# A two-block transformer layer on one core: sums over a convolution's channels by adding DMAs instead of GpSimd, and two pooling epilogues given out at two points

## The chip, the cores and the metric

The kernel runs on one core of a Trainium2 chip. The metric is the device time of one execution in microseconds (us). The engines are TensorE (PE, with its weight loads PEld), VectorE (DVE), ScalarE (ACT), GpSimd (POOL) and SyncE (SP). SP issues most DMAs; the DMAs that add to their destination are issued by POOL.

## The reference

The kernel computes two layers on 1024 positions of 1024 channels in float32. The change lies in the first one, in two of its three branches:

```
a_v, a_g, b_b, b_c, b_h, b_g, c_a, c_b, c_g, merge = split(u @ w_in + b_in)
pooled = causal_multiscale_pool(a_v)              # windows 2, 4, 8, 16, a group of 256 channels each
y_a = einsum("bsgi,gio->bsgo", pooled, pool_w) * pool_scale * silu(a_g)
h_c = causal_dwconv(c_a * sigmoid(c_b), cf_w, cf_b)           # 31 taps per channel
y_c = silu(layer_norm(h_c, cf_ln_g, cf_ln_b)) * silu(c_g)     # mean and variance over 1024 channels
m = sum over the three branches of sigmoid(merge_n) * (y_n @ w_branch[n])
```

The layer norm of `h_c` needs, for each position, the sum of `h_c` and of its square over all channels.

## The kernel before

Channels lie on partitions, 128 at a time, and positions along the free dimension, so a tile of 128x1024 is one block of 128 channels (512 KB). A float32 product is made of three products of split operands (`hilo`: a rounded part, cast by ACT, and a rest, subtracted by DVE; `mm3`). The host program writes every engine's queue in the order in which its calls are made; each engine then runs its queue in that order and waits where data or a buffer is not ready. A buffer that is used again is waited for by the next user's instruction.

The projections of the first layer run in two ways. The blocks j = 0 to 4 of the branches B and C are plain products (`slot_u`). All later projections go two blocks at a time through `run_two`, which makes seven half-size products out of eight (products 1, 6, 5, 2, 7, 3, 4 in that order, 12 matmuls each) and combines the results in PSUM by a copy on ACT and additions on DVE. ACT's copy `c1 = nc.scalar.copy(e[:, 0], banks[1])`, L456, takes the first product out of its bank. The fourth product writes that bank again and so waits for the copy; in the trace the copy is `two<-pp`. Work of the previous pair (its epilogue, `g.todo`, called `later` in the function) and of the background queue `bgq` is given out by `fill()`, which `run_two` calls after each product. A `Task` with a step k is not given out before k products have been made (`step * STEP > now[1] + 0.01`); it waits at the head of the list.

The convolution of a channel block j is done by DVE: `head`, L725, starts the tile `h`, and 30 `tap`s, L162, add to it. Then `stats()` stores `h`, squares it on ACT into a tile of the tag `e` (`sq`), and POOL adds `h` to `hs` and `sq` to `hq` (L740, L741). For j = 0 POOL copies instead. After j = 7 SP stores both sums to `st_sp` (L743, L744), from where they are read when the layer norm is due. The tag `e` is a small ring for results on the way to memory: two buffers (`n_e` = 2) while the convolutions run, one while the poolings run (`open_a` sets `n_e` = 1). The epilogues of projections (`epi_store`) use it too: an activation into `e`, L156, then a store.

The pooling products of a group g (`pool_slot`, g = 3, 2, 1, 0) are two PSUM pairs; their epilogues `one(0)` and `one(1)` scale a pair on ACT into a tile `e` and store it to `ya_sp`. For g = 0 they run at once and use other buffers, for the other three they are left to the next pair of `run_two`. In the last stage of the second layer, `down()` already uses adding DMAs on POOL (L1976, 256 KB each, from HBM).

Of the kernel before, what the change touches and what calls it, by code (L numbers as in the profile page):

```python
# [14 lines left out]
ALU = mybir.AluOpType  # L15
# [91 lines left out]
class Kernel:  # L107
# [603 lines left out]
    def block1(self):  # L711
        nc, I = self.nc, self.I
# [7 lines left out]
        def conv_tasks(j, p):  # L720
            w = lambda k: self.par("cf_w", j * 31 + k)

            def head():
                h = T["h"] = self.c0.tile([P, 1024], F, tag="h", name="h", bufs=2)
                nc.vector.tensor_scalar(h, p[:, 30:1054], w(30), self.par("cf_b", j),  # L725
                                        ALU.mult, ALU.add)

            def tap(k):
                self.stt(T["h"], p[:, k:k + 1024], w(k), T["h"], ALU.mult, ALU.add)

            def stats():
                h = T["h"]
                nc.sync.dma_start(h_sp[j], h)
                sq = e_tile()
                self.act(sq, h, AF.Square)
                if j == 0:
                    nc.gpsimd.tensor_copy(self.hs, h)
                    nc.gpsimd.tensor_copy(self.hq, sq)
                else:
                    nc.gpsimd.tensor_tensor(self.hs, self.hs, h, ALU.add)  # L740
                    nc.gpsimd.tensor_tensor(self.hq, self.hq, sq, ALU.add)  # L741
                if j == 7:
                    nc.sync.dma_start(st_sp[0], self.hs)  # L743
                    nc.sync.dma_start(st_sp[1], self.hq)  # L744

            self.bgq.append(Task(0.7, head))
            for k in range(30):
                self.bgq.append(Task(1.3, lambda k=k: tap(k)))
            self.bgq.append(Task(0, stats))

        def e_tile():
            return self.c1.tile([P, 1024], F, tag="e", name="e", bufs=self.n_e)
# [111 lines left out]
        pairs = Pairs(self.pair_tiles(lambda: self.cw, 1, True), lambda: None, lambda: None)  # L864
# [92 lines left out]
        def pool_slot(g):  # L957
            s = {}

            def pre():  # L960
                while self.bgq:
                    self.bgq.popleft()()
                pairs.flush()
                if g == 0:
                    self.open_right("ws")
                    self.resume()
                    self.dma_ahead()
                    for j in range(4):
                        split_y(1, j)
                    self.split_ahead(1)  # L970

            def mm():
                wh, wl = T["pwr"]
                s["ps"] = [self.pair(), self.pair()]
                for c in range(2):
                    for h in range(2):
                        hs = slice(h * H, (h + 1) * H)
                        for k in range(2):
                            ph, pl = T["pool", 2 * g + k]
                            ks = slice((k * 2 + c) * P, (k * 2 + c + 1) * P)  # L980
                            self.mm3(s["ps"][c][:, hs], (wh[:, ks], wl[:, ks]), (ph[:, hs], pl[:, hs]),
                                     k == 0, k == 1)

            def one(c):
                if g:
                    e = e_tile()
                else:
                    e = self.c1.tile([P, 1040], F, tag="s", name="s", bufs=2)[:, 0:1024]
                self.act(e, s["ps"][c], AF.Identity, scale=self.par("pool_scale", 2 * g + c))
                (nc.sync if g else nc.gpsimd).dma_start(ya_sp[2 * g + c], e)  # L990

            def epi():
                pairs.todo = [Task(0, lambda c=c: one(c)) for c in range(2)]
                if g == 0:
                    pairs.flush()

            self.slots.append(Slot([], mm, epi, pre=pre, name="pool%d" % g))

        def open_a():
# [35 lines left out]
        def split_y(n, j):  # L1035
            if ("Y", n) not in T:
                open_y(n)
            self.hilo(T["Y", n][0][:, j], T["Y", n][1][:, j], T["ld"].pop((n, j)))
# [1190 lines left out]
```

## Time and profile before

| what | before |
|---|---|
| median of 3 runs | 2711.1 us (2710.7 to 2712.61) |
| the profiled execution's own time | 2704.81 us |
| its span | 2703.0 us |
| mean granted TensorE clock | 0.994 |
| busy: PE, DVE, ACT, POOL | 97%, 70%, 36%, 7% of the span |

The span is the time from the first to the last instruction of the profiled execution. Busy shares are means over stages with different limits. The plain products of the first layer run up to about 376 us, the pairs of the first layer from there to about 1040 us.

### The profile page before, as it was taken

The page shows a single profiled execution, that of the slowest core. Times are in us where ns is not written, and L with a number is a line of the kernel's source. Part 1 is how long each engine was busy: PE and PEld are TensorE (multiplying, and loading weights), DVE is VectorE, ACT ScalarE, POOL GpSimd, SP SyncE. Part 2 cuts the span into 40 slices and gives each one's busy share as a digit, 9 for nine tenths or more (in the row PEclk, how much of TensorE's full clock was granted, in tenths as well). Part 3 has the DMA queues.
Part 4 walks back from the last instruction along what each step waited for, and adds up shares of the span by engine and source line. Part 5 has one row for each costly group of instructions (what it writes and reads, how often), then busy time and mean ns, then how long its engine had stood idle before and what let it go on. Part 6 is the DMA issues. An engine that isn't in the chain of part 4 may idle for free.

```text
span 2703.0 us, 29526 instructions
## 1 busy us (share of the span) xinstructions
PE 2622.2 (97%) x11688; PEld 2143.6 (79%) x11688; DVE 1881.6 (70%) x2141; ACT 981.1 (36%) x1284; POOL 182.4 (7%) x178
## 2 busy tenths in 40 slices
PE   5999999999999997999999999999999999999998
PEld 3888887888788776877887788888888888887776
DVE  7789988899886664566564254546647788885576
ACT  5322233333343333222243255542323334343333
POOL 4000000000000000000032100000000000000220
PEclk9999999999999998999999999999999999999999
DMA  6111121222232225676342121112532222216964
GB/s 234 55 63 63 63 86 70 102 86 94 86 129 109 99 108 186 255 287 253 125 156 83 68 86 65 68 32 100 180 130 78 86 79 85 88 61 234 276 147 149
DMA packets 102380, 324.63 MB, mean 120 GB/s; under 512 B 11489, under 2 KB 12001, under 8 KB 102242
## 3 DMA queue, kind: packets, MB, share of 16 engines
q1 hardware_dynamic: 95474, 309.65, 31.9%
q0 software_dynamic: 6768, 13.11, 2.6%
q8 instruction: 91, 1.49, 0.2%
q14 instruction: 47, 0.39, 0.0%
HBM read 247.21 MB, written 75.50 MB: 119 GB/s over the span
## 4 chain that ended last, share of the span: by engine, by line
PE 75%; DVE 10%; DMA 7%; ACT 4%; issue 3%; SPq 1%; POOL 1%; DVEq 0%; ACTq 0%; POOLq 0%
PE pp L143 73%; DMA A<-g_sp 1%; DVE h L162 1%; DMA B<-x_sp 1%; DVE sums L159 1%; DVE ld L159 1%; DVE wl L159 1%; DVE A L159 1%; PE pm L143 1%; DVE g L159 1%; DVE B L159 1%; ACT e L156 1%; PE pp L146 1%; PE pm L146 1%; DMA mg_sp<-e 1%
## 5 line engine op out<-in xcount | busy, mean ns | idle before, releaser
L143 PE MATMUL pp<-A,wh 128*128 128x512 f32 x2432 | 769.7, 392 | 13.5 <-DVE A L159 9.0
L143 PEld LDWEIGHTS pp<-A,wh 128*128 128x128 f32 x2432 | 454.4, 188 | 115.1 <-DVE A L159 10.9
L143 PE MATMUL pp<-A,wl 128*128 128x512 f32 x1296 | 506.0, 390 | 2.8 <-DVE wl L159 2.8
L143 PE MATMUL pp<-B,A 128*128 128x512 f32 x1676 | 487.8, 390 | 1.2 <-DVE B L159 1.1
L143 PE MATMUL pp<-A,w 128*128 128x512 f32 x1664 | 443.4, 392 | 12.8 <-DVE pp L159 6.7
L143 PEld LDWEIGHTS pp<-A,w 128*128 128x128 f32 x1664 | 313.7, 189 | 83.3 <-DVE pp L159 10.3
L143 PE MATMUL pp<-B,w 128*128 128x512 f32 x1136 | 374.7, 389 | 0.0
L143 PEld LDWEIGHTS pp<-B,A 128*128 128x128 f32 x1676 | 313.9, 188 | 68.1 <-DVE B L159 2.3
L162 DVE SCALAR_TENSOR_TENSOR h<-p,par_t,h 128x1024 f32<-128x1024 f32 x240 | 312.8, 1303 | 4.7
L143 PEld LDWEIGHTS pp<-A,wl 128*128 128x128 f32 x1296 | 243.8, 188 | 55.4 <-DVE wl L159 4.5
L143 PE MATMUL pp<-B,wh 128*128 128x512 f32 x800 | 263.8, 395 | 15.6 <-ACT B L165 8.3
L159 DVE TENSOR_TENSOR wl<-wr,wh 128x1024 fp32r<-128x1024 f32 (+1 forms) x120 | 144.3, 1203 | 172.7 <-ACT wh L165 168.8
L143 PEld LDWEIGHTS pp<-B,w 128*128 128x128 f32 x1136 | 213.2, 188 | 44.3
L143 PEld LDWEIGHTS pp<-B,wh 128*128 128x128 f32 x800 | 151.3, 190 | 49.3 <-ACT B L165 9.2
L165 ACT CAST wh<-wr 128x1024 fp32r<-128x1024 f32 (+1 forms) x120 | 118.5, 989 | 188.3 <-PE pp L143 159.2
L162 DVE SCALAR_TENSOR_TENSOR z<-pp,par_t,z 128x1023 f32<-128x1023 f32 x88 | 112.6, 1280 | 48.0 <-ACT z L156 47.0
L143 PE MATMUL pp<-yh,xh 128*128 128x512 f32 x308 | 122.6, 398 | 5.9 <-ACT yh L165 5.9
L373 ACT CAST w<-raw 128x1024 fp32r<-128x1024 f32 x50 | 52.6, 1053 | 207.8 <-PE pp L143 141.0
L143 PE MATMUL pp<-yl,xh 128*128 128x512 f32 x308 | 123.1, 400 | 4.4 <-DVE yl L159 4.4
L143 PE MATMUL pp<-A,A 128*128 128x512 f32 x324 | 126.7, 391 | 0.1
L143 PE MATMUL pp<-B,wl 128*128 128x512 f32 x320 | 125.9, 393 | 0.0
L143 PE MATMUL pp<-yh,xl 128*128 128x512 f32 x308 | 121.1, 393 | 0.0
(278 smaller groups left out, 3187.4 us busy)
## 6 DMA issues: line engine op xcount, KB each, us to landing
raw<-in_w_in SPq DMA_DIRECT2D x66, 512.0 KB, 4.1
wr<-in_w_in SPq DMA_DIRECT2D x63, 512.0 KB, 3.5
raw<-in_w_up SPq DMA_DIRECT2D x34, 512.0 KB, 5.2
mg_sp<-e SPq DMA_DIRECT2D x24, 512.0 KB, 4.1
wr<-in_w_br SPq DMA_DIRECT2D x24, 512.0 KB, 5.9
g<-mg_sp SPq DMA_DIRECT2D x24, 512.0 KB, 5.4
A<-g_sp SPq DMA_DIRECT2D x44, 256.0 KB, 6.3
g_sp<-z SPq DMA_DIRECT2D x21, 512.0 KB, 3.0
```

What stands on the lines that cost most here:

```text
L143: return self.nc.tensor.matmul(*a, **k)
L146: self.nc.tensor.transpose(*a)
L156: return self.nc.scalar.activation(out, in_, func, **kw)
L159: return self.nc.vector.tensor_tensor(out, a, b, op)
L162: self.nc.vector.scalar_tensor_tensor(out, a, s, b, op0, op1)
L165: self.nc.scalar.copy(hi, src)
L373: self.nc.scalar.copy(t.__dict__[which][0], src)
```

## The change

For j = 1 to 7 the two additions on POOL become two DMAs, issued by POOL, that read `h` or `sq` in SBUF and add it to `hs` or `hq` in SBUF. The two epilogues of a pooling get the steps 1 and 2: the first may be given out after one product of the next pair, the second after two.

```diff
                     nc.gpsimd.tensor_copy(self.hs, h)
                     nc.gpsimd.tensor_copy(self.hq, sq)
                 else:
-                    nc.gpsimd.tensor_tensor(self.hs, self.hs, h, ALU.add)
-                    nc.gpsimd.tensor_tensor(self.hq, self.hq, sq, ALU.add)
+                    nc.gpsimd.dma_start(self.hs, h, accum_op=ALU.add)
+                    nc.gpsimd.dma_start(self.hq, sq, accum_op=ALU.add)
                 if j == 7:
                     nc.sync.dma_start(st_sp[0], self.hs)
                     nc.sync.dma_start(st_sp[1], self.hq)
...
             def epi():
-                pairs.todo = [Task(0, lambda c=c: one(c)) for c in range(2)]
+                pairs.todo = [Task(0, lambda c=c: one(c), c + 1) for c in range(2)]
                 if g == 0:
                     pairs.flush()
```

ACT's queue at the start of the pair behind the pooling g = 2. The activations into `e` are `one(0)` and `one(1)`, the copy of L456 is `c1`, and the casts make weights of this pair and the next:

```order
 L373 CAST w_2393<-sums 128x1024 [waits PE_49]
 L156 ACTIVATE e<-pp,par_t 128x1024 [waits DMAHW6_49,PE_49,Activation_49]
-L156 ACTIVATE e<-pp,par_t 128x1024 [waits DMAHW7_49,PE_49,Activation_49]
-L456 COPY two<-pp 128x512 [waits PE_49]
+L456 COPY two<-pp 128x512 [waits PE_49]
+L156 ACTIVATE e<-pp,par_t 128x1024 [waits DMAHW7_49,Activation_49]
 L373 CAST w_2391<-raw 128x1024 [waits DMAHW3_49,PE_49]
 L373 CAST A_201<-sums 128x1024 [waits DVE_49]
```

The copy now stands ahead of `one(1)`; `one(0)` keeps its place. The poolings g = 3 and g = 1 read alike.

POOL's queue at the convolution blocks 1 and 2 (`q` and `p` are small memsets for the next blocks; a wait on DMASW is one for a DMA that POOL issued):

```order
 L780 MEMSET q 128x2 [waits Pool_49]
 L765 MEMSET p 128x30
-L740 TENSOR_TENSOR hs<-hs,h 128x1024 [waits DVE_49,Pool_49]
-L741 TENSOR_TENSOR hq<-hq,e 128x1024 [waits Activation_49,Pool_49]
+L740 DMA hs<-h 128x1024 [waits DVE_49,Pool_49]
+L741 DMA hq<-e 128x1024 [waits Activation_49,Pool_49]
 L780 MEMSET q 128x2 [waits Pool_49]
 L765 MEMSET p 128x30
-L740 TENSOR_TENSOR hs<-hs,h 128x1024 [waits DVE_49,Pool_49]
-L741 TENSOR_TENSOR hq<-hq,e 128x1024 [waits Activation_49,Pool_49]
+L740 DMA hs<-h 128x1024 [waits DMASW0_49,DVE_49]
+L741 DMA hq<-e 128x1024 [waits DMASW1_49,Activation_49]
```

Each addition is replaced at its place; from the second block on, a DMA also waits for the DMA that added to the same sum before.

ACT's queue at the pair behind block 5 (the two activations into `e` are the epilogue of two `merge` projections, the copy is `c1` of the pair):

```order
 L156 ACT_TABLE_LOAD [waits DMAHW5_49,DVE_49]
 L156 ACTIVATE e<-pp,par_t 128x1024 [waits Activation_49]
-L156 ACTIVATE e<-pp,par_t 128x1024 [waits Pool_49]
+L156 ACTIVATE e<-pp,par_t 128x1024 [waits DMASW1_49,Activation_49]
 L456 COPY two<-pp 128x512 [waits PE_49]
 L373 CAST w_2391<-raw 128x1024 [waits DMAHW7_49,PE_49]
```

Nothing moves here; the second activation's buffer held the square of block 5, and it is now released by the DMA's landing instead of POOL.

## Rows read from the trace of the kernel before

**Rows 1.** The page's first part: busy time, share of the span, instructions.
```profile
PE 2622.2 (97%) x11688; PEld 2143.6 (79%) x11688; DVE 1881.6 (70%) x2141; ACT 981.1 (36%) x1284; POOL 182.4 (7%) x178
```

**Rows 2.** What PE waited for, 82 to 1060 us: total, times, longest.
```profile
PE pp L143 <- DVE pp L159: 6.7, 4, 3.6
...
PE pp L143 <- ACT two L456: 5.9, 4, 2.4
```

**Rows 3.** Chain that ended last, 928 to 952 us: start, duration, what.
```profile
941.16 2.59 DMA ya_sp<-e
...
944.87 0.59 ACT two L456
```

**Rows 4.** PE's timeline behind the three poolings: start, duration, instruction, idle before.
```profile
880.30 3.04 PE L143 MATMUL pp<-A,w 128*128 128x512 f32 x12 [0.72 <-ACT two L456]
...
945.50 3.02 PE L143 MATMUL pp<-A,w 128*128 128x512 f32 x12 [2.27 <-ACT two L456]
...
1010.80 3.02 PE L143 MATMUL pp<-A,w 128*128 128x512 f32 x12 [2.39 <-ACT two L456]
```

**Rows 5.** POOL's timeline at convolution block 4.
```profile
463.25 2.42 POOL L740 TENSOR_TENSOR hs<-hs,h 128x1024 f32<-128x1024 f32 x1 [101.18 <-DVE h L162]
465.61 3.39 POOL L741 TENSOR_TENSOR hq<-hq,e 128x1024 f32<-128x1024 f32 x1
```

**Rows 6.** DVE's timeline: at block 4, and the same forms at 577 and 881 us.
```profile
463.69 3.06 DVE L159 TENSOR_TENSOR sums<-raw 128x1024 f32<-128x1024 f32 x1
466.67 2.94 DVE L725 TENSOR_SCALAR h<-p,par_t 128x1024 f32<-128x1024 f32 x1
...
577.55 0.80 DVE L725 TENSOR_SCALAR h<-p,par_t 128x1024 f32<-128x1024 f32 x1
...
881.49 1.22 DVE L159 TENSOR_TENSOR sums<-raw 128x1024 f32<-128x1024 f32 x1
```

**Rows 7.** PE's timeline behind the blocks 4, 5 and 6.
```profile
472.79 7.36 PE L143 MATMUL pp<-A,w 128*128 128x512 f32 x24 [3.62 <-DVE pp L159]
...
570.09 5.60 PE L143 MATMUL pp<-A,w 128*128 128x512 f32 x24
...
581.64 3.01 PE L143 MATMUL pp<-A,w 128*128 128x512 f32 x12 [0.51 <-ACT two L456]
...
688.40 3.90 PE L143 MATMUL pp<-A,w 128*128 128x512 f32 x9 [1.80 <-DVE pp L159]
```

**Rows 8.** One window by engine: length, busy and count each, granted clock, DMA.
```profile
472.50:476.50 4.00, 3.71 (x10) 2.96 (x11) 3.70 (x5) 0.00 (x0) 0.00 (x0) 0.63 0.00 0
```

**Rows 9.** The tile t of the last stage: duration in ns, least, median, most.
```profile
L1976 POOL DMA_DIRECT2D t<-in_w_dn x11: 865/875/1350, 2560.2 to 2611.3; - x11
...
L159 DVE TENSOR_TENSOR yl<-t,yh x11: 682/685/689, 2595.6 to 2625.8; 128x512 fp32r<-128x512 f32 x11
```

**Rows 10.** SP's issues behind convolution block 7.
```profile
799.11 0.32 SPq L744 DMA_DIRECT2D st_sp<-hq  x1
807.41 0.81 SPq L349 DMA_DIRECT2D raw<-in_w_in  x2
```

**Rows 11.** DMA queues: packets, MB, share of 16 engines' span.
```profile
q1 hardware_dynamic: 95474, 309.65, 31.9%
q0 software_dynamic: 6768, 13.11, 2.6%
```

**Rows 12.** POOL's DMA issues, 2587 to 2590 and 2473 to 2476 us: size, us to landing.
```profile
t<-in_w_dn POOLq DMA_DIRECT2D x1, 256.0 KB, 4.4
...
g_sp<-z POOLq DMA_DIRECT2D x1, 512.0 KB, 8.2
```

**Rows 13.** ACT's timeline behind block 5 (the first row is its square).
```profile
570.67 1.07 ACT L156 ACTIVATE e<-h 128x1024 f32<-128x1024 f32 x1 [4.00 <-issue]
...
578.99 2.12 ACT L156 ACTIVATE e<-pp,par_t 128x1024 f32<-128x1024 f32 x2
```

**Rows 14.** ACT's timeline behind block 4.
```profile
478.27 1.28 ACT L156 ACT_TABLE_LOAD   x1
```

## The prediction

> **What bounds the kernel now.** The first view is the page: TensorE (PE) is busy for 97% of the span [rows 1], so a change can pay only where PE stands still, or where it brings a stop of its own. The second view is the list of what PE waited for, cut to 82 to 1060 us, the stretch in which everything that the diff touches runs. Two causes matter there [rows 2]: 6.7 us for a VectorE (DVE) addition into `pp`, and 5.9 us for ScalarE's (ACT's) copy into `two`, the copy `c1` of `run_two`. The third and fourth views tell which stops these are.
>
> The copy first. In the chain that ended last, at 941 us, one reads a store `ya_sp<-e` and then the copy [rows 3]: the copy stands in ACT's queue behind the second pooling epilogue, that one waits until the first one's store has landed, because `e` has one buffer here, and PE waits for the copy. It happens after the three poolings g = 3, 2, 1, with idle times of 0.72, 2.27 and 2.39 us [rows 4].
>
> Now the addition. While GpSimd (POOL) adds `hs` and `hq`, for 2.42 and 3.39 us in the instance at 463 us [rows 5], two DVE instructions that begin meanwhile take 3.06 and 2.94 us; the same forms take 1.22 and 0.80 us elsewhere [rows 6]. So POOL's additions cost DVE (3.06 - 1.22) + (2.94 - 0.80) = 3.98 us here. PE then waits 3.62 us, and its next 24 matmuls take 7.36 us where 24 others take 5.60 [rows 7]: the granted clock is 0.63 over those 4 us, a mean of the levels 2.4 and 1.2 GHz [rows 8]. PE has the same pattern at 688 us, behind the channel block two later: 1.80 us idle, and 9 matmuls in 3.90 us [rows 7]. In the blocks 1 to 3 the additions run beside plain products, and the list has no such wait there.
>
> **The change part by part.** (a) *The two epilogues at two points.* The first stays where it was, ahead of the copy; the second goes behind the copy. The last matmul before the stop ends at 945.50 - 2.27 = 943.23 us [rows 4]. The first epilogue has ended by 941.16, when the store of its result begins [rows 3]; the copy of 0.59 us, whose product PE has computed long before, then ends near 941.8, 1.4 us before PE wants it. So the three idle times go: 0.72 + 2.27 + 2.39 = **5.4 us**. The second epilogue still waits for that store to land, at 941.16 + 2.59 = 943.75, and ends some 1.1 us later; behind it on ACT stands a cast into the buffer that PE reads in the fourth product, which begins at 943.2 and takes half of 5.60 us, so the cast can't start before 946 anyway, and nobody waits. SP issues its store at the same point of its queue as before.
>
> (b) *Fourteen additions leave POOL.* Seven pairs go, of which PE feels three. At 463 us: the DVE chain comes 3.98 us earlier, more than the 3.62 us of waiting, and with the idle time the slower clock goes: 3.62 + (7.36 - 5.60) = **5.4 us**. At 688 us: 9 matmuls at 5.60/24 = 0.233 us would be 2.1, so 1.80 + (3.90 - 2.10) = **3.6 us**. At 581 us the stop is 0.51 us [rows 7]; it is in (d). The margin at 463 us is 0.4 us, which is thin: I count the whole gain and put a smaller one among the rivals.
>
> (c) *Fourteen DMA issues come to POOL.* An issue of an adding DMA takes POOL 0.87 us, against the 2.4 to 3.4 us of an addition, and the eleven two-input DVE subtractions of the last stage, beside which such issues run, stay between 0.682 and 0.689 us [rows 9]. So I count no stretch of DVE. What stands behind them on POOL (the small memsets of `q`, `p`, `v`) comes earlier. On SP, the stores of `st_sp` now wait for landings instead of additions; the next issue in SP's queue, a load of `raw`, comes 8.3 us behind the second of them [rows 10], and that much lateness is covered.
>
> (d) *A later release of `e`.* `e` has two buffers here, and the square in one of them is now free when the DMA `hq<-e` has landed, not when POOL has added it. Who waits is an ACT activation, and in the blocks 4 to 7 the copy for PE stands right behind it. When does it land? No row shows an adding DMA of 512 KB between two places in SBUF. Its transfer time from the queues' totals [rows 11]: the hardware queue moved 309.65 MB in 31.9% of the span, so 0.524 MB take 1.46 us; the software queue 13.11 MB in 2.6%, 70.3 us; three plain 512 KB stores in it are 1.57 MB or 4.4 us, so adding costs 65.9 us for 11.5 MB, or **2.99 us** for 0.524 MB, twice a copy. Its fixed time lies between 4.4 - 1.5 = 2.9 us (an adding DMA of 256 KB after POOL had paused 25 us) and 8.2 - 1.46 = 6.7 us (a plain 512 KB DMA, the first after a long pause) [rows 12]. `hq` follows `hs` in one queue, so with T as the end of the block's convolution it lands between T + 2.9 + 6.0 = T + 8.9 and T + 6.7 + 6.0 = T + 12.7. The operation is that of the first row, the long pause before it that of the second; I take the middle, T + 10.8.
>
> The shortest way from T to such an activation is behind T = 570.67 us [rows 13]. PE wants the copy at 581.64 - 0.51 = 581.13 [rows 7]; the copy takes 0.59 and one of the two activations 1.06, so the second activation has to start at 579.48, T + 8.8. With T + 10.8 PE waits 2.0 us in place of 0.51: **-1.5 us**. The next case is the block at 463 us: the table load that now carries the wait stood 15.0 us behind T and comes 5.4 us earlier, at T + 9.6 [rows 14]. Load, activation and copy take 3.0 us, from 478.27 to 481.3; PE wants the copy two products, 5.6 us, after its 24 matmuls end at 480.15 [rows 7], so there are 4.4 us of reserve, and a landing by T + 14 costs nothing. I take the same for the two blocks behind 581 us, whose order is alike.
>
> The sum: 5.4 + 5.4 + 3.6 - 1.5 = 12.9 us. The profiled execution took 2704.8 us (span 2703.0), which gives 2691.9. The median of the runs shown, 2711.1, lies 6.3 us above the profiled one; moved by that, the forecast is **2698 us**. With the bounds of the landing: T + 8.9 leaves 0.1 us at 581 and gives 2696; T + 12.7 leaves 3.9 us there and, if the clock falls with it, 1.8 more, and gives 2702.
>
> The Trainium skill has another price for the landing ("DMA: Bandwidth & Descriptors", Anatomy of one DMA): 2.0 us and the bytes at 436 GB/s, so two of 512 KB would have landed some 4.4 us after the first issue, an estimate by that page. The 4.4 us of half the size in [rows 12] speak against it. By it nothing waits at 581 us, and the sum is 14.9 us.
>
> **The rivals.** *The landing is late, and the change loses.* Place: the activations behind `e`. From T + 8.8 each microsecond is lost once, and from about T + 14 in three places, with up to 1.8 us of slow clock at each; at T + 16 it is 7.2 + 2 x 2.0 + 3 x 1.8 = 16.6 us against gains of 5.4 + 5.4 + 3.6 + 0.5 = 14.9. It decides from T + 15.4. At T + 20 the time is 2711.1 + 11.2 + 12 + 5.4 - 14.9 = 2725 us. For it: no row shows this form. Against it: the rate would have to be half of that in the queue's totals, or the fixed time 9.4 us. 8%. The Trainium skill names a way to it ("SBUF — State Buffer", SBUF: two separate sides): GpSimd can't write its DMA descriptors while DVE runs an instruction that holds both ports. The `h` start of 0.80 us is the one such candidate near T.
>
> *DVE isn't relieved.* If issuing held DVE as adding does, 2 x 0.87 of the 3.98 us would stay; 463 us would keep 1.4 us of idle time, and perhaps its slow clock: 2701 us. Against it stand the subtractions of [rows 9]. 8%.
>
> *DVE was only the last of several.* PE's stops at 463 and 688 us are taken over by another wait, and what stays is (a): 2711.1 - 5.4 = 2706 us, at the edge of no change. For it: the thin margin. 9%.
>
> **How the numbers follow.** The forecast with its bounds, 2696 to 2702, has 75%. A measurement of this kernel can tell 0.2%, 5.4 us, from no change. Forecast and the second rival are faster: 83%. The third is the same: 9%. The first is slower: 8%. For 8 times in 10, 2694 to 2706: 2 us under the lower bound, for small stops that DVE's lateness may cause elsewhere and that I don't count, and up to the third rival.
>
> **What would show it.** In the changed profile: no idle time of PE after the three poolings, and the copy ahead of the second epilogue; no DVE instruction over 1.5 us beside the sums' DMAs; PE idle under 0.5 us at the places of 473 and 688 us, and full clock; landings of `hq<-e` between 8 and 12 us after the start of `hs<-h`. The prediction is wrong if PE waits for the copy at several blocks behind an activation that a software DMA released, or if DVE is stretched still.

## The result

| kernel | median of the runs | lowest to highest |
|---|---|---|
| before | 2711.3 us (4 runs) | 2710.7 to 2712.61 |
| changed | 2690.4 us (4 runs) | 2689.41 to 2693.45 |

The ratio is 0.9924, with a 95% interval of 0.9907 to 0.9941: 0.8% faster, 20.9 us by the medians. The forecast was 2698 us with a range of 2694 to 2706, so the sign is right and the gain was sized too small; the time lies 3.6 us under the range.

The profiled execution of the changed kernel took 2690.44 us. Against the first profiled execution of before, 2704.81 us, that is 14.4 us, close to the 12.9 us of the sum. So the working from the rows and the runs disagree by some 6 us, and most of this section and the next is about those.

First the views that answer to the rows of before. What PE waited for from 82 to 1045 us in the changed kernel (total, times, longest; compare [rows 2]):

```profile
PE pp L143 <- ACT two L456: 1.3, 1, 1.3
PE pp L143 <- DVE pp L159: 1.3, 2, 0.7
```

The copy took 5.9 us of PE's time in four stops, now one stop is left; the DVE addition took 6.7 us in four stops, of which the two long ones are gone. VectorE's timeline at block 4 shows why the second number fell (compare [rows 6]):

```profile
463.35 1.21 DVE L159 TENSOR_TENSOR sums<-raw 128x1024 f32<-128x1024 f32 x1
464.49 0.81 DVE L725 TENSOR_SCALAR h<-p,par_t 128x1024 f32<-128x1024 f32 x1
465.21 1.41 DVE L159 TENSOR_TENSOR sums<-sums,raw 128x512 f32<-128x512 f32 x2
```

The two instructions that took 3.06 and 2.94 us beside GpSimd's additions now take 1.21 and 0.81 us beside the issue of two DMAs. PE goes on without a stop, and its 24 matmuls take the ordinary time, where [rows 7] has 7.36 us behind 3.62 us of idle time:

```profile
468.69 5.64 PE L143 MATMUL pp<-A,w 128*128 128x512 f32 x24
```

The pooling g = 2, in ACT's timeline: the first epilogue, the copy for PE, and the second epilogue, which waits for the store as before, but behind the copy:

```profile
931.51 1.12 ACT L156 ACTIVATE e<-pp,par_t 128x1024 f32<-128x1024 f32 x1 [1.80 <-DMA mg_sp<-e]
932.53 0.57 ACT L456 COPY two<-pp 128x512 f32<-128x512 f32 x1
935.77 1.12 ACT L156 ACTIVATE e<-pp,par_t 128x1024 f32<-128x1024 f32 x1 [2.66 <-DMA ya_sp<-e]
```

The new wait, behind block 5, in ACT's timeline (compare [rows 13]), and PE's row next to it:

```profile
564.93 1.06 ACT L156 ACTIVATE e<-h 128x1024 f32<-128x1024 f32 x1 [4.00 <-issue]
...
575.08 1.11 ACT L156 ACTIVATE e<-pp,par_t 128x1024 f32<-128x1024 f32 x1 [4.56 <-DMA hq<-e]
576.09 0.58 ACT L456 COPY two<-pp 128x512 f32<-128x512 f32 x1
```

```profile
576.72 0.50 PE L143 MATMUL pp<-A,w 128*128 128x512 f32 x1 [1.33 <-ACT two L456]
```

The second activation waits 4.56 us for the landing of `hq<-e`, and PE waits 1.33 us for the copy behind it, in place of 0.51 us. It is the only block where this reaches PE. The landing, in the list of DMA issues from 565 to 567 us (size, us to landing):

```profile
hs<-h POOLq DMA_DIRECT2D x1, 512.0 KB, 5.4
hq<-e POOLq DMA_DIRECT2D x1, 512.0 KB, 8.6
```

`hq<-e` was issued at 566.39 (POOL's timeline), so it landed at 575.0, 10.1 us behind the start of the square; over the seven blocks it was 7.9 to 11.9, and 7.7 to 11.6 from the issue of `hs<-h`. The late landings are those beside which the hardware queue moved much. Between its issue and its landing that queue moved 0.2 to 0.4 MB in four blocks, where `hq<-e` took 6.5 to 6.9 us, and 0.8 to 1.3 MB in the other three, where it took 8.5 to 10.5 us. The two ends, from the issue of `hs<-h` to the landing of `hq<-e` (queue: packets, MB, share of the transfer engines; then size and us to landing), are block 4, 463 to 471 us:

```profile
q1 hardware_dynamic: 144, 0.52, 17.1%
...
hq<-e POOLq DMA_DIRECT2D x1, 512.0 KB, 6.5
```

and block 3, 352 to 364.2 us:

```profile
q1 hardware_dynamic: 432, 1.57, 42.4%
...
hq<-e POOLq DMA_DIRECT2D x1, 512.0 KB, 10.5
```

No run varies that traffic alone, so the connection is seen and not tested. At the end, SP's stores of the sums and the load behind them (compare [rows 10]):

```profile
791.12 0.32 SPq L743 DMA_DIRECT2D st_sp<-hs  x1
793.67 0.32 SPq L744 DMA_DIRECT2D st_sp<-hq  x1
...
798.44 0.81 SPq L349 DMA_DIRECT2D raw<-in_w_in  x2
```

The second store is issued 4.8 us ahead of the load instead of 8.3. No stop of PE follows from it.

### The profile page after: what moved, and what is told of

Same layout as the page of the kernel before. It is cut to its first block, busy times and chain, and to the rows that moved or that the text cites. A ratio compares the mean times of both kernels' runs of the same rounds, so it can differ in the third digit from the quotient of the medians.

```text
span 2688.6 us, 29545 instructions
## 1 busy us (share of the span) xinstructions
PE 2618.4 (97%) x11688; PEld 2142.2 (80%) x11688; DVE 1861.9 (69%) x2141; ACT 980.6 (36%) x1284; POOL 157.4 (6%) x178
## 4 chain that ended last, share of the span: by engine, by line
PE 63%; issue 15%; DMA 9%; DVE 9%; ACT 3%; SPq 1%; POOL 1%; DVEq 0%; ACTq 0%; POOLq 0%
PE pp L143 61%; DMA ld<-h_sp 1%; DVE h L162 1%; DMA A<-g_sp 1%; DMA B<-x_sp 1%; DMA hs<-h 1%; DVE wl L159 1%; DVE g L159 1%; PE pm L143 1%; DVE A L159 1%; PE pp L146 1%; DVE sums L159 1%; PE pm L146 1%; DVE B L159 1%; DMA adag<-in_ada 1%
```

## The experiments

To compare executions without their start and end, I use one more number: the time from the start of matmul 1900 to the start of matmul 4300 (counted from 0 in order of time; there are 11688 in each kernel, in the same order). This stretch, from 465 to 1029 us of the first trace, holds the blocks 4 to 7 and the three poolings. From the trace of every profiled execution:

```
execution      whole, us   stretch, us   from there to the start of the last matmul, us
before          2704.81      563.7         1669.2
again           2707.58      564.9         1670.8
again_b         2714.99      568.8         1674.4
again_c         2714.10      566.1         1675.5
again_d         2712.68      566.6         1671.7
changed         2690.44      549.0         1669.9
after_b         2693.45      549.0         1672.2
after_c         2690.28      548.8         1669.6
steps_only      2697.48      555.7         1670.1
dmas_only       2698.49      556.8         1670.1
hq_first        2691.10      546.6         1673.0
hq_first_b      2689.23      546.4         1671.1
no_sums         2686.53      546.3         1668.4
```

**The kernel before again** (label again; no edit):

> The kernel before, unchanged, for a second profile of it: the timed runs of before lie at 2711 us, its profiled execution at 2704.8, and the changed kernel's own runs and profile both at 2690. Theory A (the stops that the change removes are longer in most executions than in the profiled one, by slow clock behind more of them): the new profile takes about 2711 us, and PE's stops and slow matmuls between 460 and 1015 us sum to some 21 us instead of 15. Theory B (the stops are the same, and some 6 us lie elsewhere in the program): the stops at 473, 581, 688, 880, 945 and 1011 us sum to 15 us as before, and the rest is found in another stage. Theory C (the first profile was of a chip or an execution that was 6 us faster in everything): 2705 or 2711 us with no place that stands out.

Its 10 runs had a median of 2710.76 us (2707.42 to 2714.82), beside 2709.5 us of 18 runs of the kernel before in the same comparison. The profiled one took 2707.58 us, and its stretch is 1.2 us longer than in the first profile. That decides little, since this execution is again one of the shortest.

**One part alone.** The steps without the DMAs, and the DMAs without the steps:

```diff
-                pairs.todo = [Task(0, lambda c=c: one(c)) for c in range(2)]
+                pairs.todo = [Task(0, lambda c=c: one(c), c + 1) for c in range(2)]
```

> The sums stay on GpSimd, only the two pooling epilogues are given out at two points. By the sum of the prediction 5.4 us less than before: no idle time of PE behind the three poolings, the stops at 473 and 688 us stay, 2705.9 us. Theory A allows up to 5.4 us more (slow clock behind three stops): 2700 to 2706. If the copy was not what PE waited for there: 2711.

```diff
-                    nc.gpsimd.tensor_tensor(self.hs, self.hs, h, ALU.add)
-                    nc.gpsimd.tensor_tensor(self.hq, self.hq, sq, ALU.add)
+                    nc.gpsimd.dma_start(self.hs, h, accum_op=ALU.add)
+                    nc.gpsimd.dma_start(self.hq, sq, accum_op=ALU.add)
```

> The sums go to adding DMAs, the pooling epilogues stay as before. By the traces of before and after: 5.6 us at 473, 4.0 at 688, less 0.8 at 577, so 9 us less than before: 2702 us, and the stops of 0.7, 2.3 and 2.4 us behind the poolings stay. Theory A: 2699 to 2702. If issuing the DMAs held VectorE as adding did: 2709 or more.

The steps alone: 2698.3 us, ratio 0.9965 (0.9952 to 0.9978), which is under the 2700 to 2706 us that theory A allowed. The DMAs alone: 2701.1 us, ratio 0.9969 (0.9959 to 0.9979), within the 2699 to 2702 us. What PE waited for between 460 and 1020 us, with the steps alone:

```profile
PE pp L143 <- DVE pp L159: 5.9, 3, 3.6
...
PE pp L143 <- ACT two L456: 0.5, 1, 0.5
```

and with the DMAs alone:

```profile
PE pp L143 <- ACT two L456: 6.9, 4, 2.4
...
PE pp L143 <- DVE pp L159: 0.5, 1, 0.5
```

Each part removes its own stops and leaves the other's; nothing is given back between them. By the medians the steps brought 11.2 us and the DMAs 8.4 us, where the rows of before gave 5.4 and 7.5. The intervals of the two ratios, 6.0 to 13.0 us and 5.7 to 11.1 us, hold the 7.5 and don't hold the 5.4, by little. So more came from the steps than the idle times hold, as theory A says; how much more, these medians don't tell.

**More profiles of both** (labels again_b, again_c, again_d, after_b; no edit):

> The kernel before, one more profiled execution: its runs spread from 2704 to 2715 us, so one profile says little of the median. Theory A (slow clock behind the stops that the change removes comes and goes): an execution near 2711 us has the same stops between 460 and 1015 us, 14 to 15 us, but the granted clock is low behind three or more of them, 3 to 6 us more than in the first profile. Theory B: between 460 and 1015 us it is like the first profile within 1.5 us, and what it is longer than 2704.8 us lies in another stage.

> The kernel before, one more profiled execution, with the same two theories and the same numbers as for the one ahead of it.

> The kernel before, one more profiled execution, with the same two theories and the same numbers as for the two ahead of it.

> The changed kernel, one more profiled execution. Theory A: between 460 and 1015 us it has one stop of 1 to 2 us and hardly any slow clock, as in its first profile, and 2689 to 2693 us. Theory B: the stage that makes executions of the kernel before long makes this one long too, now and then.

These three executions of before took 2715.0, 2714.1 and 2712.7 us, the changed one 2693.45, all on one chip, and not the chip of the label again. In all three, PE's stops behind the poolings g = 2 and g = 1 are followed by a low clock, which was not so in the first profile. PE's timeline of again_b (compare [rows 4], where the same 12 matmuls take 3.02 us):

```profile
946.55 4.50 PE L143 MATMUL pp<-A,w 128*128 128x512 f32 x12 [2.25 <-ACT two L456]
...
1014.25 4.62 PE L143 MATMUL pp<-A,w 128*128 128x512 f32 x12 [3.27 <-ACT two L456]
```

The windows of again_b show it in the granted clock (the column behind the five engines'; the first row is the stop of block 4):

```profile
471.00:479.00 8.00, 6.26 (x15) 5.02 (x16) 5.84 (x7) 1.80 (x3) 0.00 (x0) 0.57 0.22 62
...
946.00:950.00 4.00, 3.44 (x9) 2.72 (x10) 3.40 (x5) 0.50 (x2) 0.00 (x0) 0.57 0.32 131
1014.00:1018.00 4.00, 3.75 (x10) 2.97 (x11) 3.71 (x5) 0.19 (x1) 0.00 (x0) 0.58 0.59 197
```

The same places of the first profile:

```profile
945.00:949.00 4.00, 3.50 (x15) 2.92 (x16) 3.45 (x5) 1.11 (x2) 0.00 (x0) 1.00 0.32 131
1010.00:1014.00 4.00, 3.20 (x14) 2.66 (x15) 3.15 (x5) 1.12 (x3) 0.00 (x0) 1.00 0.56 197
```

A clock of 0.57 to 0.58 over 4 us is a mix of 1.2 and 2.4 GHz; 12 matmuls then take 1.5 to 1.6 us longer. Behind block 4 the clock is low in all five profiles of before, for a longer time in two of them. In the changed kernel's three profiles no matmul of the stretch runs at the low clock. The stretch is 563.7 to 568.8 us in the five profiles of before, mean 566.0, and 548.8 to 549.0 in the three of the changed kernel: a gain of 17.1 us, where the first profile alone shows 14.7. Theory A holds for these 2.3 us; of the 3 to 6 us that it gave to each long execution, only again_b has as much (5.1), the other two have 2.4 and 2.9. Theory B holds for others: again_b is 5.1 us longer behind the stretch than the first profile, again_c 6.3, again_d 2.5, and after_b is 2.3 us longer there than the changed kernel's first. So the part that the change doesn't touch varies by some 6 us from one execution to the next, and the first profile of before was the shortest of the five in both parts. Theory C, a first execution that was shorter in everything, isn't needed for the stretch, where the rows show the places; for the rest it is not decided.

**The other order of the two DMAs**, and the changed kernel without them. The first as a diff against the changed kernel:

```diff
-                    nc.gpsimd.dma_start(self.hs, h, accum_op=ALU.add)
                     nc.gpsimd.dma_start(self.hq, sq, accum_op=ALU.add)
+                    nc.gpsimd.dma_start(self.hs, h, accum_op=ALU.add)
```

> The changed kernel with the two adding DMAs in the other order, hq<-e ahead of hs<-h. If the later release of e is what is left of a cost, hq<-e lands about 7 us after the convolution block's end instead of 10, the activation behind block 5 waits for nothing that PE feels, and PE's stop of 1.3 us at 577 us goes: 1.3 us less than the changed kernel, 2689 us. If the two DMAs share the transfer engines so that both land late: no change, 2690.4.

It had 2688.74 us, ratio 0.9927 (0.9912 to 0.9942). ACT's timeline behind block 5 in this kernel:

```profile
564.80 1.06 ACT L156 ACTIVATE e<-h 128x1024 f32<-128x1024 f32 x1 [4.00 <-issue]
...
572.60 1.12 ACT L156 ACTIVATE e<-pp,par_t 128x1024 f32<-128x1024 f32 x1 [2.20 <-DMA hq<-e]
573.61 0.58 ACT L456 COPY two<-pp 128x512 f32<-128x512 f32 x1
```

The wait for the landing is 2.20 us instead of 4.56, the copy is done at 574.2, and PE's fourth product starts at 575.10 without a stop:

```profile
575.10 2.88 PE L143 MATMUL pp<-A,w 128*128 128x512 f32 x12
```

`hq<-e` now lands 7.7 us after the start of the square, as expected, so the two DMAs don't both land late. Then a comparison on one chip, with a third kernel that leaves the fourteen DMAs out, so that its sums hold the first channel block alone:

```diff
-                else:
-                    nc.gpsimd.dma_start(self.hs, h, accum_op=ALU.add)
-                    nc.gpsimd.dma_start(self.hq, sq, accum_op=ALU.add)
```

> The changed kernel again, for a comparison on one chip with the two below and with the kernel before. 2690 to 2693 us; the stretch from the 1900th to the 4300th matmul at 549 us as in its two profiles, against 564 to 569 us in five profiles of the kernel before.

> The square's DMA ahead of the other one, again. Its first profile had the stretch between the 1900th and the 4300th matmul 2.4 us shorter than the changed kernel. If that is the order's doing: 2.4 us less than the changed kernel here, 2688 to 2690 us, and again no stop for the copy near 575 us. If it was chance: the same time as the changed kernel within 1 us.

> The changed kernel without the fourteen adding DMAs: the sums for the layer norm of the convolution hold the first channel block alone. It is the bound of what freeing GpSimd can bring. If the DMAs cost only the stop at 577 us: the same as with the square's DMA first, some 2.4 us less than the changed kernel, 2688 us. If they also cost by sharing the transfer engines or VectorE's ports: 2 us or more below that, 2686 us or less.

The changed kernel had 2690.07 us (ratio 0.9930, 0.9917 to 0.9943), the other order 2689.23 (0.9926, 0.9913 to 0.9938), no DMAs 2688.69 (0.9926, 0.9913 to 0.9939), before 2708.43 us (11 runs). Those three medians can't be told apart: 0.8 us between the two orders fits "the same within 1 us" as well. The stretch can: 548.8, 546.4 and 546.3 us, and the other profiles of either order lie within 0.3 us of these. With the other order and without the sums, the list of what PE waited for between 460 and 1020 us has this one row, a stop of before that no part of the change touches:

```profile
PE pp L143 <- DVE pwr L159: 0.9, 1, 0.9
```

So the adding DMAs as the change issues them cost 2.5 us: 1.7 around the copy behind block 5, and 0.8 around a second stop, 47 us later, in the changed kernel's PE timeline:

```profile
623.88 3.47 PE L143 MATMUL pp<-A,w 128*128 128x512 f32 x14 [0.54 <-DVE pp L159]
```

The chain that ended last there leads back, through DVE's queue and a load of `raw`, to that copy and to the landing of `hq<-e`. Before has this stop too, 0.55 us behind its 0.51 us for the copy, and the prediction didn't count it. That is why the other order brought 2.4 us of stretch where 1.3 were expected. In the other order the DMAs cost 0.1 to 0.3 us, and that is as good as having no sums at all. It is the better kernel by the stretch, by 0.1% of the time.

## Why the prediction was right and wrong

(a) *The two epilogues* was right in place and order: the copy is ahead of the second epilogue, and the three stops are gone. Its size was wrong: 5.4 us was the idle time of one execution. From matmul 3000 to 4300, which holds block 7 and the three poolings, the kernel before takes 302.7, 303.2, 306.9, 306.7 and 305.9 us, mean 305.1, and the changed one 296.4 to 296.7: it measured 8.5 us. The kernel with the steps alone takes 296.4 there, and the one with the DMAs alone 304.4, so it is the steps' doing. Of the 3.1 us above the idle times, 1.8 on the mean are low clock behind two of the stops (1.3 to 1.6 us each), which was there in three of five executions and not in the one from which the term was taken; 0.5 are longer stops (5.4 to 6.5 us in the five). For the stop at 473 us the prediction did count the clock, because the row showed it.

(b) *Fourteen additions leave POOL* and (c) *fourteen DMA issues come* were right, in mechanism and nearly in size. DVE is not stretched beside the issues, so the second rival fell; in the rows that spoke against it, seven of the eleven subtractions ran beside an issue, not all. No other wait took over the stops at 463 and 688 us, so the third rival fell too. For matmuls 1900 to 2400, with the stops of the blocks 4 and 5, the sum was 5.4 - 1.5 = 3.9 us; by the means of the profiles it is 120.3 - 115.4 = 4.9. For 2400 to 3000, the stop behind block 6, it was 3.6, and is 140.7 - 136.9, 3.7 before rounding.

(d) *A later release of `e`* was right in mechanism, and its number came out partly by luck. The landing was put at T + 10.8 with bounds of 8.9 and 12.7: it came at T + 10.1 where it mattered, and PE waited 1.3 us where 2.0 were forecast. But in four of the seven blocks it landed at T + 7.9 to T + 8.6, under the lower bound. The upper bound took the 8.2 us of a plain DMA for the price of a long pause. In the window of that row, 2473 to 2476 us of before, the hardware queue held nearly all of the transfer engines' time:

```profile
q1 hardware_dynamic: 289, 1.04, 95.6%
```

And `hs<-h`, which in the changed kernel is the first after a pause of 60 to 110 us each time, landed 4.9 to 5.5 us after its issue in five of seven blocks, 2.0 to 2.6 us more than its 2.9 us of transfer. So the pause isn't seen to cost anything, and block 5, one of the three blocks with more traffic beside, came near the middle of the bounds for another reason than the one they were made from. The transfer time of 2.99 us can be checked too: the software queue grew by 7.34 MB and from 2.6 to 4.1% of the span, 40 us for fourteen DMAs, 2.9 us each. The first rival, the late landing, needed T + 15.4; the latest was T + 11.9. The way to it that the prediction names isn't seen at block 4, where the `h` start of 0.81 us began 0.1 us behind the issue of `hq<-e`: that one landed after 6.5 us, among the earliest. The price in the Trainium skill ("DMA: Bandwidth & Descriptors", Anatomy of one DMA), by which both would have landed 4.4 us after the first issue, an estimate by that page, doesn't agree with these landings; for adding DMAs in SBUF the measured 7.7 to 11.6 us decide.

The step that failed is the last one of the sum: "The median of the runs shown, 2711.1, lies 6.3 us above the profiled one; moved by that, the forecast is **2698 us**". It took the distance for a constant that the changed kernel would have as well. It isn't one. The first profile was the shortest of five executions of before: of its distance, 2.3 us on the mean were stops and low clock at the very places that the change removes, and 3.1 us (1672.3 on the mean against 1669.2) were variation of the rest, which hits any kernel. The changed kernel's runs lie at 2688.6 to 2693.5 us, around its profile and not 6 us above it. Behind the same step stands the sum's size: 12.9 us were forecast, the stretch gave 17.1 on the mean, and 3.1 of the missing 4.2 us are (a). Without the shift the sum itself gave 2691.9 us, 1.5 us from the result, but that would have been luck: the profile it starts from is 6.5 us under the median, and the gain is 8.0 us short of 20.9. With the shift the stated range missed by 3.6 us.

That the low clock behind the poolings' stops belongs to the gain is shown: it is in the rows of three executions of before, and behind g = 1 in the one with the DMAs alone, which keeps these stops; it is in none of the changed kernel. In PE's timeline with the DMAs alone:

```profile
1001.99 4.41 PE L143 MATMUL pp<-A,w 128*128 128x512 f32 x12 [2.41 <-ACT two L456]
```

Why it follows the same stop in one execution and not in another stays open. The three executions of before ran on one chip, and the chip may have a part in it; but on each of two other chips the runs of before spread as widely, 2704.0 to 2714.8 and 2705.4 to 2715.3 us, with granted clocks of 0.991 to 0.995.

The mean granted clock of most runs is on record, and it carries this beyond the traces. It is 0.9930 on the mean of 43 runs of before and 0.9955 on that of ten of the changed kernel. What that leaves short of full speed is 18.8 and 12.1 us, 6.7 us apart. The traces place the difference: behind the stretch the low clock lasts about as long in both kernels (20.5 to 27.3 us in the five profiles, 20.5 to 30.7 in the three), in the stretch it lasts 6.8 to 17.1 us in before and is absent from the changed kernel. The stops themselves are 12.4 us of idle time on the mean of the five profiles and 1.9 of the three, 10.5 us apart. So, as an estimate, 17.2 of the 19.1 us between the means of these runs are idle time and low clock. The other 2 us, and with them a gain of 1 to 3 us behind the stretch (1672.3 us on the mean against 1670.5, where single executions vary by 6), are neither shown nor excluded.

## What to carry to other kernels

One profile is one execution: before its time is set against a median, look at how far the runs of the kernel spread, and price the stops in the rows with and without the low clock that may follow them; a kernel with many short stops spreads more (2704 to 2715 us here) than one without (2689 to 2693). An engine that is 7% busy can still cost time, through the engine that it holds up while it works: look for instructions of one form with two durations. And where a buffer is freed by a DMA instead of an engine, issue first the DMA for whose source buffer somebody waits. Before a time to landing is taken over from another row, look at what else the DMA engines moved beside it.

## What the runs showed of the hardware

A stop of TensorE of 2.3 us behind the pooling g = 2 was followed by the low clock in three executions and by the full clock in two of the same program; where it came, it cost 1.5 to 1.6 us, two thirds of the stop once more. An adding DMA from SBUF to SBUF of 512 KB took 2.9 us of transfer time, twice the 1.46 us of the hardware queue's mean for as many bytes, and the second of two in a row landed 7.7 to 11.6 us after the first was issued, later the more the hardware queue moved beside it. VectorE's one-input start of `h`, not only its two-input instructions, was held beside GpSimd's addition (2.94 against 0.80 us) where it began second; where it began first, at 208 and 353 us, it took 0.81 us and the addition 2.8 instead of 2.4. Neither kind was held beside the issue of a DMA by GpSimd.
